# Linear attention on one core: K and V in rows of 8 KB, V loaded straight into its blocks, the first matmul 128 wide

## The chip, the cores and the metric

The kernel runs on one core of a Trainium2 chip. The metric is device time in microseconds (us) of one execution. The engines are TensorE (PE; its weight loads are listed as PEld), VectorE (DVE), ScalarE (ACT), GpSimd (POOL) and SyncE (SP). POOL and SP issue the transfers (DMA).

## What is computed

```python
# Q, K, V: (8, 12, 512, 64) float32
Q_feat = np.maximum(0, Q) + 1
K_feat = np.maximum(0, K) + 1
KV = np.einsum('bhkd,bhkv->bhdv', K_feat, V)
K_sum = np.sum(K_feat, axis=2)
numerator = np.einsum('bhqd,bhdv->bhqv', Q_feat, KV)
denominator = np.einsum('bhqd,bhd->bhq', Q_feat, K_sum)
return numerator / (denominator[:, :, :, None] + 1e-10)
```

There are 96 heads (8 x 12) of 512 rows of 64 numbers. Each of Q, K, V and the output is 12.6 MB. For every head a 64x64 matrix KV and a vector K_sum of 64 are formed, and then each query row is multiplied by them and divided.

## The kernel before

**Tiling.** The inputs are read as a list of rows, and a partition of the on-chip memory gets several successive rows. For K and V a partition gets 16 rows (`C2`, 4 KB in HBM) of each of two or four chunks, for Q 32 rows (`C4`, 8 KB). With 16 rows a partition, 32 partitions hold one head, and a chunk of 128 partitions holds four heads. A *group* g (12 of them, `NG`) is two such chunks, eight heads; a *pair* s is two groups, 16 heads, for which one DMA each loads K, V and Q (1 MB as landed, since the loads turn four-byte numbers into two-byte ones on their way; `load`, line 106, and `load_q`, line 112). The first K goes over SP without conversion (`load_first_k`, line 93).

**First product.** A matmul contracts over the partitions, and 128 partitions hold four heads. To keep the heads apart, V is spread: `v_all` has, for each row, four blocks of 64 columns, of which partition 32b..32b+31 fills only block b and holds zeros in the others, and four columns of ones in the same pattern for K_sum. The zeros are written once (`clear`, lines 240 to 242). `v_blocks` copies each loaded V into its blocks with four copies of 32 partitions, three on DVE (line 155) and one on ACT (line 153). `k_features` forms max(K+1, 1) on DVE (line 137). `keys_values` (line 171) runs, for each of the 16 rows, two matmuls of 64 stationary columns and 260 moving ones: chunk 0 goes to PSUM partitions 0 to 63, chunk 1 to 64 to 127. ACT copies the result out into `kva_all` (lines 181 and 182), in which the two heads that share a column block stand on a diagonal with zeros beside them.

**Queries.** `q_features` (line 137 again, two instructions a group) and `transposes` (line 192: 16 matmuls with an identity a group, in two PSUM tiles, each copied out by ACT at line 195; one of them by DVE near the end).

**Output.** `output(g)` is two halves; in each, 16 matmuls (line 205) write two PSUM tiles of eight, and DVE normalises each tile with a reciprocal (line 222) and a multiplication (line 223) into `o_sb`. Stores of 1 MB (`store`) go over POOL (line 126), the last three over SP (lines 129 and 132).

**Order.** All is written out by hand under `tc.manual_schedule()`: each engine runs its instructions in the order of the program text, and waits for the others by semaphores. In the loop over g, the features and V blocks of group g come before the output of group g-2, then the transposes or Q features, the product of g, and on odd g the loads of the pair after next. Two buffers each for K, V and Q (`IN_BUFS`) set when a load can be issued: the buffer's last reader has to be done. POOL issues its transfers one after the other in that order, and one queue serves them. There are two PSUM tiles each for the product, the output and the transposes, so the third output tile waits until the first has been normalised.

Of the kernel before, what the change touches and what calls it, by code (L numbers as in the profile page):

```python
# [8 lines left out]
FP32 = mybir.dt.float32  # L9
BF16 = mybir.dt.bfloat16  # L10
ALU = mybir.AluOpType

BANK = 512
IN_BUFS = 2
OUT_BUFS = 3
LAG = 3
# [3 lines left out]
def kernel(  # L20
# [10 lines left out]

# [3 lines left out]
    P = 128  # L43
    C = 8
    C2 = 2 * C
    C4 = 4 * C
    R = 4
    NPAIR = B * H * S // (P * C)
    NP = 4
    NG = NPAIR // NP  # L50
    D1 = D + 1
    W = 2 * D1

    def view(t, c):
        return t.flatten_outer_dims().rearrange("(n p c) d -> p n c d", p=P, c=c)

    q_eights = view(Q, C4)
    k_dram = view(K, C2)
    v_dram = view(V, C2)
# [3 lines left out]
    head_pool = ctx.enter_context(tc.tile_pool(name="head_pool", bufs=1))  # L63
    in_pool = ctx.enter_context(tc.tile_pool(name="in_pool", bufs=IN_BUFS))
    kf_pool = ctx.enter_context(tc.tile_pool(name="kf_pool", bufs=2))
    qf_pool = ctx.enter_context(tc.tile_pool(name="qf_pool", bufs=3))
# [8 lines left out]
    NV = 4  # L75
    v_all = const.tile([P, 2, 2, C2, 4 * D1], BF16, name="v_all")
    ones = const.tile([P, 4], BF16, name="ones")
    zero = const.tile([P, 1], FP32, name="zero")
    kva_all = const.tile([P, NV, 4, 2, D1], BF16, name="kva_all")
    kva_diag = [kva_all[:, i] for i in range(NV)]  # L80

    drams = dict(k=k_dram, v=v_dram)
    raw = {}
    bufs = {}
# [4 lines left out]
    cells_of = {}  # L89

    def load_first_k():
        k_raw = head_pool.tile([P, 2, C2, D], FP32, name="k_first")
        nc.sync.dma_start(out=k_raw, in_=k_dram[:, 0:4:2])
        raw["k", 0] = k_raw

    def load(x, groups):
        s = groups[0] // 2
        if groups[0] % 2 == 0 or (x, s) not in bufs:
            bufs[x, s] = in_pool.tile([P, 4, C2, D], BF16, name=f"{x}_raw")
        if len(groups) == 2:  # L100
            ms = slice(0, 4)
            of = slice(4 * s, 4 * s + 4)
        else:
            ms = slice(groups[0] % 2, 4, 2)
            of = slice(4 * s + groups[0] % 2, 4 * s + 4, 2)
        nc.gpsimd.dma_start(out=bufs[x, s][:, ms], in_=drams[x][:, of])  # L106
        for g in groups:
            raw[x, g] = bufs[x, s][:, g % 2 : 4 : 2]

    def load_q(s):  # L110
        t = in_pool.tile([P, 2, C4, D], BF16, name="q_raw")
        nc.gpsimd.dma_start(out=t, in_=q_eights[:, 2 * s : 2 * s + 2])  # L112
        rows = t.rearrange("p n (r c) d -> p n r c d", c=C)
        for e in range(2):
            raw["q", 2 * s + e] = rows[:, :, :, 4 * e : 4 * e + 4]

    def load_pair(s):
        load("k", (2 * s, 2 * s + 1))
        load("v", (2 * s, 2 * s + 1))
        load_q(s)  # L120

    def store(g):
        s = g // 2
        o_to = o_dram[:, 2 * NP * s : 2 * NP * s + 2 * NP]
        if g < NG - 2:
            nc.gpsimd.dma_start(out=o_to[:, g % 2 : 2 * NP : 2], in_=outs[s][:, g % 2 : 2 * NP : 2])  # L126
            return
        if g == NG - 2:
            nc.sync.dma_start(out=o_to[:, 0 : 2 * NP : 2], in_=outs[s][:, 0 : 2 * NP : 2])
            return  # L130
        for h in range(2):
            nc.sync.dma_start(
                out=o_to[:, 2 * h + g % 2 : 2 * NP : NP], in_=outs[s][:, 2 * h + g % 2 : 2 * NP : NP]
            )

    def feature(dst, src):
        nc.vector.tensor_scalar(  # L137
            out=dst, in0=src, scalar1=1.0, scalar2=1.0, op0=ALU.add, op1=ALU.max
        )

    def k_features(g):
        k_raw = raw.pop(("k", g))
        kf = kf_pool.tile([P, C2, 2, D], BF16, name="kf")
        for n in range(2):
            feature(kf[:, :, n], k_raw[:, n])
        kfs[g] = kf

    def v_blocks(g):
        v_raw = raw.pop(("v", g))
        for b in range(4):  # L150
            ps = slice(32 * b, 32 * b + 32)
            if b == 3:
                nc.scalar.copy(out=v_all[ps, g % 2, :, :, b * D : b * D + D], in_=v_raw[ps])  # L153
            else:
                nc.vector.tensor_copy(  # L155
                    out=v_all[ps, g % 2, :, :, b * D : b * D + D], in_=v_raw[ps]
                )

    def q_features(g):
        q_raw = raw.pop(("q", g))  # L160
        qf = qf_pool.tile([P, R, C // 2, 2, D], BF16, name="qf")
        for n in range(2):
            feature(qf[:, :, :, n], q_raw[:, n])
        qfs[g] = qf

    def keys_values(g):
        kf = kfs.pop(g)
        kva_ps = psum_kva.tile([P, 4 * D1], FP32, name="kva_ps")
        for c in range(C2):
            for n in range(2):  # L170
                nc.tensor.matmul(  # L171
                    kva_ps[64 * n : 64 * n + 64],
                    lhsT=kf[:, c, n, :],
                    rhs=v_all[:, g % 2, n, c, :],
                    start=(c == 0),
                    stop=(c == C2 - 1),
                )
        kva = kva_diag[g % NV]
        for n in range(2):
            ps = slice(64 * n, 64 * n + 64)  # L180
            nc.scalar.copy(out=kva[ps, :, n, 0:D], in_=kva_ps[ps, 0 : 4 * D].rearrange("p (b d) -> p b d", b=4))  # L181
            nc.scalar.copy(out=kva[ps, :, n, D], in_=kva_ps[ps, 4 * D : 4 * D1])  # L182

    def transposes(g):
        qf = qfs.pop(g)
        if g % 2 == 0:
            qts[g // 2] = mid_pool.tile([P, C, P, R], BF16, name="qt")
        for half in range(2):
            qt_ps = psum_qt.tile([P, 2, R, P], BF16, name="qt_ps")
            for c in range(2):  # L190
                for r in range(R):
                    nc.tensor.transpose(qt_ps[:, c, r], qf[:, r, 2 * half + c, :, :], identity)  # L192
            copy = nc.vector.tensor_copy if half and g == NG - 2 else nc.scalar.copy
            lo = g % 2 * 4 + 2 * half
            copy(out=qts[g // 2][:, lo : lo + 2], in_=qt_ps.rearrange("p c r q -> p c q r"))  # L195

    def out_matmuls(g, h):
        qt = qts[g // 2]
        kva = kva_diag[(g // 2 * 2 + h) % NV]
        ops = [psum.tile([P, 2, BANK], FP32, tag="ps", name="o_ps") for _ in range(2)]  # L200
        for c in range(C):
            for j in range(2):
                b = 2 * (g % 2) + j
                q = 16 * (4 * h + b)
                nc.tensor.matmul(  # L205
                    ops[c // 4][64 * j : 64 * j + 64, c // 2 % 2, (c % 2) * W : (c % 2) * W + W],
                    lhsT=qt[:, c, q : q + 16, :],
                    rhs=kva[:, b],
                    start=True,
                    stop=True,  # L210
                )
        cells_of[g, h] = ops

    def norms(g, h):
        ops = cells_of.pop((g, h))
        if (g % 2, h) == (0, 0):
            outs[g // 2] = out_pool.tile([P, 2 * NP, C, D], FP32, name="o_sb")
        o_sb = outs[g // 2]
        for i in range(2):
            cells = ops[i][:, :, 0 : 2 * W].rearrange("p b (c n x) -> p b c n x", n=2, x=D1)  # L220
            recip = recip_pool.tile([P, 2, 2, 2, 1], FP32, name="recip")
            nc.vector.reciprocal(out=recip, in_=cells[:, :, :, :, D:D1])  # L222
            nc.vector.tensor_tensor(  # L223
                out=o_sb[:, 2 * h + g % 2 : 2 * NP : NP, 4 * i : 4 * i + 4].rearrange(
                    "p n (b c) d -> p b c n d", b=2
                ),
                in0=cells[:, :, :, :, 0:D],
                in1=recip.to_broadcast([P, 2, 2, 2, D]),
                op=ALU.mult,
            )  # L230

    def output(g):
        for h in range(2):
            out_matmuls(g, h)
            norms(g, h)

    def clear(i):
        t = v_all[:, i].rearrange("p n c x -> p (n c x)").bitcast(FP32)
        w = t.shape[1] * 5 // 8
        nc.vector.memset(t[:, 0:w], 0.0)  # L240
        nc.scalar.copy(out=t[:, w:], in_=zero.to_broadcast([P, t.shape[1] - w]))  # L241
        nc.vector.tensor_copy(
            out=v_all[:, i, :, :, 4 * D : 4 * D1].rearrange("p n c j -> p (n c) j"),
            in_=ones[:, None, :].to_broadcast([P, 2 * C2, 4]),
        )

    with tc.manual_schedule():
        nc.vector.memset(zero, 0.0)
        load_first_k()
        load("v", (0,))  # L250
        load_q(0)
        load("k", (1,))
        load("v", (1,))
# [78 lines left out]
```

## Time and profile before

| What | Value |
|---|---|
| runs (median of 3; lowest to highest) | 126.66 us (126.54 to 127.17) |
| profiled execution, its span | 124.7 us (the page gives the span; the median of the runs lies 1.96 us above it) |
| PE busy | 61.8 us, 960 matmuls |
| DVE busy | 89.3 us |
| ACT busy | 59.6 us |
| POOL busy | 26.1 us |
| bytes over HBM | 37.75 MB read, 12.58 MB written |
| POOL's DMA queue | 10448 packets, 97.4% of 16 DMA engines' span |
| K, V, Q loads, 1 MB landed each | 22.1, 23.0, 26.0 us from issue to landing (median) |
| first K, 1 MB over SP | 4.9 us from issue to landing |

How to read the views used: the page's slices show the span in 40 equal parts, each digit the busy share in tenths (9 is 90% or more); PEclk is the clock that TensorE was granted, in tenths of full speed. The DMA share is that of the 16 DMA engines. A view of stretches gives busy us and the number of instructions for each engine in a stretch of time, then the granted clock, the DMA share and the GB/s as landed. A group line gives source line, engine, operation, output and inputs with their shapes, the count, busy us, mean ns of one, idle time before them and what ended it. In the view in order of time each line begins with the start and the length in us. Matmuls are pipelined, so that the length of one says little: the time in which 32 of them pass says more.

### The profile page before, as it was taken

The page shows a single profiled execution, that of the slowest core. Times are in us where ns is not written, and L with a number is a line of the kernel's source. Part 1 is how long each engine was busy: PE and PEld are TensorE (multiplying, and loading weights), DVE is VectorE, ACT ScalarE, POOL GpSimd, SP SyncE. Part 2 cuts the span into 40 slices and gives each one's busy share as a digit, 9 for nine tenths or more (in the row PEclk, how much of TensorE's full clock was granted, in tenths as well). Part 3 has the DMA queues.
Part 4 walks back from the last instruction along what each step waited for, and adds up shares of the span by engine and source line. Part 5 has one row for each costly group of instructions (what it writes and reads, how often), then busy time and mean ns, then how long its engine had stood idle before and what let it go on. Part 6 is the DMA issues. An engine that isn't in the chain of part 4 may idle for free.

```text
span 124.7 us, 2348 instructions
## 1 busy us (share of the span) xinstructions
PE 61.8 (50%) x960; PEld 50.7 (41%) x960; DVE 89.3 (72%) x191; ACT 59.6 (48%) x86; POOL 26.1 (21%) x51
## 2 busy tenths in 40 slices
PE   0004945200692838539684691069495267775300
PEld 0003735200581827428573490058384155663100
DVE  4895444206999899997999930699959699969700
ACT  7532289306039781956639462601993295450000
POOL 6991023100011630233302420302020200020000
PEclk9999999955589999995999689756999958997555
DMA  3999999999999999999999999999999999999993
GB/s 95 330 214 214 209 198 210 210 214 213 208 213 213 216 214 208 212 213 217 230 405 327 210 212 214 215 338 403 227 212 215 218 255 415 420 413 416 406 409 126
DMA packets 11803, 32.13 MB, mean 258 GB/s; under 512 B 528, under 2 KB 528, under 8 KB 11792
## 3 DMA queue, kind: packets, MB, share of 16 engines
q0 software_dynamic: 10448, 28.84, 97.4%
q1 hardware_dynamic: 1344, 3.15, 6.7%
q8 instruction: 7, 0.11, 0.3%
q14 instruction: 4, 0.03, 0.1%
HBM read 37.75 MB, written 12.58 MB: 404 GB/s over the span
## 4 chain that ended last, share of the span: by engine, by line
DMA 56%; DVE 19%; PE 8%; ACT 6%; issue 3%; POOL 2%; POOLq 0%
DMA v_raw<-in_V_dram 30%; DMA q_raw<-in_Q_dram 26%; DVE o_sb L223 8%; PE kva_ps L171 5%; DVE v_all L155 5%; ACT v_all L153 3%; DVE qf L137 2%; PE qt_ps L192 2%; DVE recip L222 2%; ACT qt L195 2%; POOL v_raw L106 1%; DVE qt L195 1%; ACT kva_all L181 1%; POOL k_raw L106 1%; DVE kf L137 1%
## 5 line engine op out<-in xcount | busy, mean ns | idle before, releaser
L205 PE MATMUL o_ps<-kva_all,qt 128*64 128x130 bf16 x384 | 20.0, 240 | 37.0 <-DVE recip L222 27.0
L171 PE MATMUL kva_ps<-v_all,kf 128*64 128x260 bf16 x384 | 29.8, 320 | 15.8 <-DVE v_all L155 15.6
L155 DVE COPY v_all<-v_raw 32x2048 bf16<-32x2048 bf16 x36 | 25.8, 717 | 13.5 <-DMA v_raw<-in_V_dram 13.1
L223 DVE TENSOR_TENSOR o_sb<-o_ps,recip 128x512 f32<-128x512 f32 x48 | 33.2, 692 | 1.6
L171 PEld LDWEIGHTS <-kf 128*64 128x64 bf16 x384 | 24.6, 130 | 19.0 <-DVE v_all L155 16.0
L205 PEld LDWEIGHTS <-qt 128*64 128x64 bf16 x384 | 14.0, 118 | 42.2 <-issue 26.0
L153 ACT COPY v_all<-v_raw 32x2048 bf16<-32x2048 bf16 x12 | 22.6, 1893 | 16.9 <-DMA v_raw<-in_V_dram 16.7
L195 ACT COPY qt<-qt_ps 128x1024 bf16<-128x1024 bf16 x23 | 22.2, 1015 | 6.8 <-PE qt_ps L192 6.5
L181 ACT CAST kva_all<-kva_ps 64x256 bf16<-64x256 f32 x24 | 8.9, 371 | 27.5 <-PE kva_ps L171 27.3
L126 POOL DMA_DIRECT2D out_dram<-o_sb x10 | 8.6, 864 | 35.9 <-DVE o_sb L223 27.2
L192 PE MATMUL qt_ps<-identity,qf 128*128 128x128 bf16 x192 | 14.8, 235 | 2.0 <-ACT qt L195 1.3
L192 PEld LDWEIGHTS <-qf 128*128 128x128 bf16 x192 | 12.4, 106 | 4.5 <-issue 2.5
L137 DVE TENSOR_SCALAR kf<-k_raw 128x1024 bf16<-128x1024 bf16 x22 | 8.5, 426 | 7.6 <-DMA k_raw<-in_K_dram 7.6
L106 POOL DMA_DIRECT2D k_raw<-in_K_dram x6 | 4.9, 822 | 35.0 <-DVE kf L137 35.0
L222 DVE RECIPROCAL recip<-o_ps 128x8 f32<-128x8 f32 x48 | 9.6, 200 | 1.4 <-PE o_ps L205 1.2
L137 DVE TENSOR_SCALAR qf<-q_raw 128x1024 bf16<-128x1024 bf16 x24 | 8.8, 431 | 2.1 <-DMA q_raw<-in_Q_dram 2.0
L106 POOL DMA_DIRECT2D v_raw<-in_V_dram x7 | 5.4, 766 | 13.4 <-ACT v_all L153 9.3
L240 DVE MEMSET v_all<- 128x2600 f32 x2 | 4.5, 2225 | 0.9 <-issue 0.9
L112 POOL DMA_DIRECT2D q_raw<-in_Q_dram x6 | 4.3, 716 | 0.0
L182 ACT CAST kva_all<-kva_ps 64x4 bf16<-64x4 f32 x24 | 4.1, 170 | 0.0
L241 ACT COPY v_all<-zero 128x1560 f32<-128x1560 f32 x2 | 2.9, 1487 | 0.0
L261 POOL MEMSET kva_all<- 128x130 bf16 x16 | 2.4, 201 | 0.0
(13 smaller groups left out, 5.8 us busy)
## 6 DMA issues: line engine op xcount, KB each, us to landing
out_dram<-o_sb POOLq DMA_DIRECT2D x10, 1024.0 KB, 25.7
q_raw<-in_Q_dram POOLq DMA_DIRECT2D x6, 1024.0 KB, 26.0
k_raw<-in_K_dram POOLq DMA_DIRECT2D x5, 1024.0 KB, 22.1
v_raw<-in_V_dram POOLq DMA_DIRECT2D x5, 1024.0 KB, 23.0
k_first<-in_K_dram SPq DMA_DIRECT2D x1, 1024.0 KB, 4.9
v_raw<-in_V_dram POOLq DMA_DIRECT2D x2, 512.0 KB, 10.7
out_dram<-o_sb SPq DMA_DIRECT2D x1, 1024.0 KB, 7.0
out_dram<-o_sb SPq DMA_DIRECT2D x2, 512.0 KB, 6.4
```

What stands on the lines that cost most here:

```text
L106: nc.gpsimd.dma_start(out=bufs[x, s][:, ms], in_=drams[x][:, of])
L126: nc.gpsimd.dma_start(out=o_to[:, g % 2 : 2 * NP : 2], in_=outs[s][:, g % 2 : 2 * NP : 2])
L137: nc.vector.tensor_scalar(out=dst, in0=src, scalar1=1.0, scalar2=1.0, op0=ALU.add, op1=ALU.max)
L153: nc.scalar.copy(out=v_all[ps, g % 2, :, :, b * D : b * D + D], in_=v_raw[ps])
L155: nc.vector.tensor_copy(out=v_all[ps, g % 2, :, :, b * D : b * D + D], in_=v_raw[ps])
L171: nc.tensor.matmul(kva_ps[64 * n : 64 * n + 64], lhsT=kf[:, c, n, :], rhs=v_all[:, g % 2, n, c, :], start=(c == 0), stop=(c == C2 - 1),)
L181: nc.scalar.copy(out=kva[ps, :, n, 0:D], in_=kva_ps[ps, 0 : 4 * D].rearrange("p (b d) -> p b d", b=4))
L192: nc.tensor.transpose(qt_ps[:, c, r], qf[:, r, 2 * half + c, :, :], identity)
L195: copy(out=qts[g // 2][:, lo : lo + 2], in_=qt_ps.rearrange("p c r q -> p c q r"))
L205: nc.tensor.matmul(ops[c // 4][64 * j : 64 * j + 64, c // 2 % 2, (c % 2) * W : (c % 2) * W + W], lhsT=qt[:, c, q : q + 16, :], rhs=kva[:, ...
L222: nc.vector.reciprocal(out=recip, in_=cells[:, :, :, :, D:D1])
L223: nc.vector.tensor_tensor(out=o_sb[:, 2 * h + g % 2 : 2 * NP : NP, 4 * i : 4 * i + 4].rearrange("p n (b c) d -> p b c n d", b=2), in0=cell ...
```

## The change

- K and V are read with 32 rows a partition (8 KB), as Q is. A head then takes 16 partitions, a chunk eight heads, and a pair two chunks (six pairs; no groups any more).
- V is loaded by four DMAs of 32 partitions each, straight into the blocks of two large buffers (`v_bufs`, nine blocks; chunk 0 uses blocks 0 to 4, chunk 1 blocks 4 to 8). Block 4, shared, holds the four columns of ones. The copies of `v_blocks` go. The zeros are written once: five blocks by DVE, four by ACT, for each buffer.
- A block of 32 partitions now holds two heads. K's features are formed twice, for the even heads with the partitions of the odd ones at zero, and the reverse, by operands that differ per partition (`shift`, `least`, made by `masks`). The two copies are the 128 stationary columns of one matmul; the moving side is five blocks of 64, 320 columns. `keys_values` runs 32 such matmuls for each chunk, and four ACT copies pick the parts.
- The order in the loop becomes, for pair s: features and product of chunk 0, output 0 of pair s-1, features of chunk 1, Q's features, product of chunk 1, output 1 of pair s-1, loads of pair s+2, a store, the transposes of pair s. Output tiles are of 1 MB with six buffers; all stores are 1 MB, two at the end over SP.

```diff
-    q_eights = view(Q, C4)
-    k_dram = view(K, C2)
-    v_dram = view(V, C2)
+    q_dram = view(Q, ROWS)
+    k_dram = view(K, ROWS)
+    v_dram = view(V, ROWS)
...
+    v_bufs = [const.tile([P, 2 * NB - 1, ROWS, D], BF16, name=f"v_buf{i}") for i in range(2)]
+    kvas = [const.tile([P, 8, 2, D1], BF16, name=f"kva{i}") for i in range(2)]
...
+    def load_v(s):
         for b in range(4):
             ps = slice(32 * b, 32 * b + 32)
+            nc.gpsimd.dma_start(
+                out=v_bufs[s % 2][ps, b : b + NB + 1 : NB], in_=v_dram[ps, 2 * s : 2 * s + 2]
+            )
...
+    def k_features(s, n):
+        k_raw = raw.pop(("k", s, n))
+        kf = kf_pool.tile([P, ROWS, 2, D], BF16, name="kf")
+        for a in range(2):
+            nc.vector.tensor_scalar(
+                out=kf[:, :, a],
+                in0=k_raw,
+                scalar1=shift[:, a : a + 1],
+                scalar2=least[:, a : a + 1],
+                op0=ALU.add,
+                op1=ALU.max,
+            )
...
+    def keys_values(s, n):
+        kf = kfs.pop((s, n))
+        v = v_bufs[s % 2][:, n * (NB - 1) : n * (NB - 1) + NB]
+        kva_ps = psum_kva.tile([P, NB, D], FP32, name="kva_ps")
+        for c in range(ROWS):
+            nc.tensor.matmul(
+                kva_ps,
+                lhsT=kf[:, c].rearrange("p a d -> p (a d)"),
+                rhs=v[:, :, c],
...
+        for s in range(NPAIR):
+            k_features(s, 0)
+            keys_values(s, 0)
+            if s:
+                output(s - 1, 0)
+                if s > 1:
+                    store(s - 2, 1, nc.gpsimd)
+            k_features(s, 1)
+            q_features(s)
+            keys_values(s, 1)
+            if s:
+                output(s - 1, 1)
+            if s + 2 < NPAIR:
+                load_k(s + 2)
+                load_q(s + 2)
+                load_v(s + 2)
+            if s:
+                store(s - 1, 0, nc.gpsimd)
+            transposes(s, 0)
+            transposes(s, 1)
+        s = NPAIR - 1
+        store(s - 1, 1, nc.gpsimd)
+        output(s, 0)
+        store(s, 0, nc.sync)
+        output(s, 1)
+        store(s, 1, nc.sync)
```

In the start-up, `load_first_k`, `load_q(0)` and the load of K's second chunk are issued first; `load_v(0)` stands behind the clearing of the first V buffer, `load_k(1)` and `load_q(1)` behind that, and `load_v(1)` behind the clearing of the second.

## The prediction

> **What bounds the kernel now.** I read the page's slices first, then the HBM line, the chain's shares, the stretches of one kind of transfer, and last the groups and the instructions in order of time.
>
> ```profile
> PE 61.8 (50%) x960; PEld 50.7 (41%) x960; DVE 89.3 (72%) x191; ACT 59.6 (48%) x86; POOL 26.1 (21%) x51
> ...
> PEclk9999999955589999995999689756999958997555
> DMA  3999999999999999999999999999999999999993
> ...
> HBM read 37.75 MB, written 12.58 MB: 404 GB/s over the span
> ...
> DMA 56%; DVE 19%; PE 8%; ACT 6%; issue 3%; POOL 2%; POOLq 0%
> ```
>
> The DMA row is full from the second slice to the next to last, and no engine is near full: the transfers are the bound. Three stretches by kind (last column: GB/s as landed; loads land two-byte, so their HBM bytes are double), first Q (8 KB rows), then K and V (4 KB rows), then stores:
>
> ```profile
> 28.80:31.40 2.60, 0.00 (x0) 0.00 (x0) 2.23 (x4) 1.89 (x1) 0.00 (x0) 0.50 1.07 216
> 48.80:51.40 2.60, 2.46 (x48) 2.08 (x46) 2.60 (x8) 1.33 (x5) 0.00 (x0) 1.00 1.13 213
> 104.00:108.00 4.00, 2.67 (x44) 1.91 (x41) 3.93 (x10) 1.98 (x6) 0.00 (x0) 1.00 1.02 417
> ```
>
> That is 432, 426 and 417 GB/s of HBM bytes: 4 KB rows already move within 1.5% of 8 KB rows. At about 420, the 50.33 MB need 119.8 us; with the first data at 2.7 us (an estimate from the first slice) and the last store's completion, 124.7 us is full. A gain is hardly to be had there; the question is whether compute still hides under 20.0 us of DMA per pair (8.39 MB / 0.42; loads alone 15.0, K, Q and V 5.0 each, two stores 5.0).
>
> **The rows for the sum.** Groups of the page (out<-in, count, busy, mean ns), then instructions in order of time (start, us, engine, line):
>
> ```profile
> L171 PE MATMUL kva_ps<-v_all,kf 128*64 128x260 bf16 x384 | 29.8, 320 | 15.8 <-DVE v_all L155 15.6
> L155 DVE COPY v_all<-v_raw 32x2048 bf16<-32x2048 bf16 x36 | 25.8, 717 | 13.5 <-DMA v_raw<-in_V_dram 13.1
> ...
> L137 DVE TENSOR_SCALAR kf<-k_raw 128x1024 bf16<-128x1024 bf16 x22 | 8.5, 426 | 7.6 <-DMA k_raw<-in_K_dram 7.6
> ```
> ```profile
> 86.78 1.07 PE L192 MATMUL qt_ps<-identity,qf 128*128 128x128 bf16 x16
> ...
> 100.97 3.24 PE L171 MATMUL kva_ps<-v_all,kf 128*64 128x260 bf16 x32 [2.69 <-DVE v_all L155]
> ...
> 108.58 1.98 PE L171 MATMUL kva_ps<-v_all,kf 128*64 128x260 bf16 x32
> 110.39 0.62 PE L205 MATMUL o_ps<-kva_all,qt 128*64 128x130 bf16 x16
> ```
>
> What to see: the mean of 320 ns misleads, since 32 matmuls pass in 1.98 us. Two 64-wide ones run side by side, a pair in 124 ns. After an idle 2.69 us the same 32 take 3.24.
>
> **Part 1, first matmul 128 wide.** The count stays 384 (32 per half pair), but each now fills the array by itself and streams 320 columns. Pairs of 260 columns take 124 ns and pairs of 130 columns 78 (0.62 us / 8): 0.354 ns a column more, so 320 columns take 145 ns. By the transposes (1.07 us / 16 = 67 ns for 128 columns with their weight load), scaled, 167. I take 150, nearer to the same instruction: **4.8 us** per 32, bounds 4.65 and 5.35, where 1.98 stood. It can't fall below 1.98: more columns, and no partner beside it. PE's first product grows from 12 x 1.98 = 24 to 58 us.
>
> **Part 2, V into the blocks.** The copies go: 25.8 us of DVE, 12 x 1.89 of ACT. Both lay beside DMA; alone this saves nothing. V costs 24 POOL issues of about 0.7 us, against 7 now; POOL is 21% busy. The first V load now waits for the clears: memset of 5120 elements by the 2600 in 2.23 us, 4.4 us; ACT's 4096 by 1560 in 1.49, about 3.8; done near 6 us. Behind it on POOL stand k1, q1, identity, memsets and v1. The queue then still holds k_first, q0 and half of k0 until about 13 us, which covers it; without cover it would cost 3 us once. V's rate with 32 partitions is not in the trace: nothing lost is one end, half the rate (10 us a pair for V) the other. I take nothing, as the landed 213 GB/s would have to fall below 190 to show at all, other terms being longer.
>
> The Trainium skill, "SBUF — State Buffer", "Door 1: The DMA port swizzle", speaks against this: 32 partitions reach 8 of 16 ports, 189 GB/s measured for 1 MiB against 328. No row here has such a transfer. Counting landed bytes, by its 189 V would take 5.5 us a pair, hidden; counting HBM bytes it is the second rival.
>
> **Part 3, K's features twice.** 24 instructions of 2048 elements replace 24 of 1024. The copies of 2048 elements take 0.69 each: 1.4 us for a half pair, against 0.85 now. A per-partition operand may take the fast rate away; that is a rival. With Q's four (1.43, beside half 1's product) and eight normalisations at 0.84, DVE has 10.9 us a pair, under 20. The five mask instructions and the marks (some 0.06 to 0.3 each) stand on DVE before 11 us, ahead of V0's landing at 18.1, and cost nothing.
>
> **Part 4, the order.** This carries the sum. On PE, pair s runs: product of half 0, output 0 of pair s-1, product of half 1, output 1 of pair s-1, transposes of s. DVE runs output 0's normalisations and only then the features of half 1, for which PE waits. From the rows:
> - product half 0: 4.8;
> - output 0: PE starts at 110.39, the fourth normalisation ends at 114.28 (113.59 + 0.69): 3.9;
> - features of half 1: 1.4;
> - product half 1: 4.8;
> - output 1 on PE: 110.39 to the end of the fourth group at 113.08 is 2.7; its DVE rest and the next half's features (3.9 + 1.4 = 5.3) hide beside the last two terms (6.2);
> - transposes: 16 in 1.07, then ACT's copies hold two more groups of 8 (copies from 87.81, 1.93 for two): 3.5.
>
> Sum **21.1 us a pair**, above DMA's 20.0. The engines are no fuller than now; they take turns.
>
> Now the clock. The window 110.40 to 113.80 holds only spaced output matmuls and the granted clock is 0.5 after it:
>
> ```profile
> 96.00:100.00 4.00, 1.25 (x24) 1.00 1.10 216
> 100.00:104.00 4.00, 3.02 (x32) 0.57 1.03 301
> ```
>
> Here too 1.25 us of PE work in 4 is followed by the low clock, and 32 matmuls at 3.24. In the new order PE has, between the two products, 2.7 us of spaced outputs and 2.6 idle: the same thinness. I add 1.6 us a pair, half of the 3.2 us that the low clock would cover (in the trace it lasts 3.4 us when dense work follows). Bounds: 0, and 3.4 if both halves meet it. **22.7 us a pair.** The Trainium skill, "TensorE: Matmul & The Clock Gate", Part 1, has the clock judged by free-running windows of 3.4 us; the trace agrees (its clock records have low stretches of 3.41, 6.83 and 10.24 us).
>
> Loads stay ahead: V of pair s+2 is issued when half 1 of pair s is done, 15 us in, thus 30 us before use, and needs 20.
>
> **The sum.** V0 lands after the same 6.29 MB as now the second V: 18.1 us. Pair 0 has no outputs: 7.0 (4.8 and 2.2 for the low clock at PE's first work, where now 3.68 stands for 1.98) + 4.8 + 3.5 = 33.4, and V1 lands 15.0 after V0, 33.1. Five pairs: 5 x 22.7 = 113.5, to 146.9. Pair 5's outputs: eight normalisations at 0.84 with 0.8 ahead, 7.5. The last store, 1 MB on SP where two halves stand now, 4.9 (the 1 MB k_first took that from issue to landing; stores behind a backlog take 6.4 to 7.0, and here DMA is idle), 0.6 to the end. Span 159.9. The page has the profiled span, 124.7; the median of the runs, 126.66, lies 1.96 above it, which I add: **162 us**.
>
> **Rivals.**
> - *The chain of turns, forecast* (0.74): pair 20.5 (product 4.5, no low clock) to 24.5: 46.4 + 5P + 2 = 151 to 171.
> - *V at half rate* (0.10): DMA 25 us a pair exceeds 22.7. V0 23, then 20 a pair to V3 83, with stores 25 to V5 133; + 22.7 + 13.0 + 2 = 171. Against: K/V land as fast as Q, nothing suggests a limit on the SBUF side. For: no such shape in the trace.
> - *The features lose their rate* (0.07): by the four-byte row (0.78 for 1024) 3.0 instead of 1.4, pair 25, 173; by a normalisation's 692 ns for 512 elements, 5.5, pair 30, 198. Against: two scalars are already in the instruction; only their kind changes.
> - *DMA stays the bound* (0.06): the wide product costs no more than now, pair 15.5. V5 cannot land before 102.8 (2.7 + 42 MB / 0.42, four stores ahead of it), + 15.5 + 13.0 + 2 = 133; up to 138 at pair 20.
> - *Not slower* (0.03): pair 4's outputs and pair 5's features and transposes run ahead of V5. After V5 stay 4.8 + 4.8 + 7.5 + 5.5 = 22.6; with 1% off the loads 101.8 + 22.6 + 2 = 126.4. It decides only where the outputs stand before the product; in PE's stream they stand behind it.
>
> **Numbers.** Runs of this kernel can tell 0.5% from no change. Faster 0.01, within 0.5% 0.02, slower 0.97. The range 149 to 175 holds the forecast, V at half rate and the first price of the features, and leaves out about 0.12.
>
> **What would show it.** Right: DMA well under 9 tenths in the middle, all loads landed some 20 us before use, PE waiting for DVE's kf once a pair, 32 products in 4.7 to 6.5 us, pairs about 22 us apart. Wrong: a full DMA row to 120 us (DMA still bounds), GB/s near 100 in V's stretches (V's rate), k features over 1 us each (their rate), products under 3 us.

## The result, and the profile after

| | before | after |
|---|---|---|
| runs | 126.62 us median of 4 (126.54 to 127.17) | 159.25 us median of 4 (158.23 to 160.07) |
| ratio after / before | | 1.256, 95% interval 1.2505 to 1.2615: slower |
| profiled execution | 126.66 us, span 124.7 | 158.23 us, span 156.5 (1.73 us lie above the span) |
| POOL's DMA queue, share of 16 engines' span | 97.4% (10448 packets) | 77.2% (7776 packets) |
| 32 matmuls of the first product | 1.98 us at the full clock | 4.35 to 4.51 at the full clock, 6.03 to 7.33 in half 1 |

From the page after: busy times, the rows of clock and DMA over 40 slices of 3.9 us, the bytes, the shares of the chain that ended last, and the two groups that the change made longer: the first product and K's features.

```profile
PE 96.7 (62%) x960; PEld 65.3 (42%) x960; DVE 76.9 (49%) x159; ACT 41.6 (27%) x75; POOL 36.6 (23%) x69
...
PEclk9999999999959999559999699997589998799955
DMA  5999999999999999999999799999910702403376
...
HBM read 37.75 MB, written 12.58 MB: 322 GB/s over the span
...
PE 42%; DVE 30%; DMA 10%; ACT 7%; issue 3%; POOL 3%; ACTq 1%
...
L137 PE MATMUL kva_ps<-v_buf,kf 128*128 128x320 bf16 x384 | 66.4, 342 | 32.1 <-DMA v_buf<-in_V_dram 18.3
...
L109 DVE TENSOR_SCALAR kf<-k_raw,shift,least 128x2048 bf16<-128x2048 bf16 x22 | 17.4, 835 | 6.2 <-PE kva_ps L137 6.2
```

The bytes are those of before. But for the first slice and one of 7 tenths, the DMA row is full for 29 slices, to 113 us, and then it is mostly empty: by then the loads are done, and what is left waits for the engines. In the chain DMA fell from 56% to 10%, PE rose from 8% to 42% and DVE from 19% to 30%. None of the engines is near full, so they wait for one another. How, the chain shows for one pair (start, length, engine, tile, line; the lines left out are the steps between):

```profile
54.67 4.35 PE kva_ps L137 x32
59.02 0.37 PE o_ps L173 x8
...
62.16 0.69 DVE o_sb L183
62.85 1.46 DVE kf L109 x2
...
64.36 7.33 PE kva_ps L137 x32
71.69 0.37 PE o_ps L173 x8
...
74.33 0.57 PE qt_ps L160 x8
...
74.97 1.94 ACT qt L161 x2
...
77.56 4.35 PE kva_ps L137 x32
```

From 54.67 to 77.56 the end is handed on without a gap: product of half 0, output with its normalisations, K's features of half 1 (half n is the pair's chunk n), product of half 1 (7.33 where the one before took 4.35), output, transposes, next product. No DMA stands in it.

The same pair in order of time on PE: the idle time in brackets and what ended it.

```profile
54.51 4.51 PE L137 MATMUL kva_ps<-v_buf,kf 128*128 128x320 bf16 x32
58.95 0.64 PE L173 MATMUL o_ps<-kva,qt 128*64 128x130 bf16 x16
60.48 0.42 PE L173 MATMUL o_ps<-kva,qt 128*64 128x130 bf16 x8 [0.90 <-DVE recip L182]
61.23 0.42 PE L173 MATMUL o_ps<-kva,qt 128*64 128x130 bf16 x8 [0.33 <-DVE o_sb L183]
64.36 7.33 PE L137 MATMUL kva_ps<-v_buf,kf 128*128 128x320 bf16 x32 [2.71 <-DVE kf L109]
```

Between the products PE has 1.48 us of work in 5.3 (0.64 + 0.42 + 0.42), and the clock's records show one low stretch a pair, 3.41 or 6.83 us long, that begins there.

The stretches of one kind of transfer (last columns: granted clock, DMA share, GB/s as landed), first Q or K, then V's four DMAs of 32 partitions; then two of 10 us late in the span:

```profile
18.40:22.60 4.20, 4.20 (x19) 2.40 (x18) 0.10 (x1) 0.00 (x0) 1.63 (x3) 1.00 1.07 215
28.20:32.20 4.00, 2.56 (x35) 2.12 (x34) 0.00 (x0) 3.11 (x7) 2.13 (x4) 1.00 1.06 210
```
```profile
104.00:114.00 10.00, 5.97 (x43) 3.37 (x38) 6.18 (x14) 0.66 (x4) 0.75 (x1) 0.68 0.97 343
114.00:124.00 10.00, 7.76 (x95) 5.66 (x93) 4.85 (x10) 4.64 (x8) 0.75 (x1) 0.98 0.27 102
```

V moves at 210 GB/s landed, 420 of HBM bytes, against 215 and 430 for the other loads. From 114 to 124 us DMA is at a quarter.

### The profile page after: what moved, and what is told of

Same layout as the page of the kernel before. It is cut to its first block, busy times and chain, and to the rows that moved or that the text cites. A ratio compares the mean times of both kernels' runs of the same rounds, so it can differ in the third digit from the quotient of the medians.

```text
span 156.5 us, 2331 instructions
## 1 busy us (share of the span) xinstructions
PE 96.7 (62%) x960; PEld 65.3 (42%) x960; DVE 76.9 (49%) x159; ACT 41.6 (27%) x75; POOL 36.6 (23%) x69
## 3 DMA queue, kind: packets, MB, share of 16 engines
q0 software_dynamic: 7776, 28.84, 77.2%
## 4 chain that ended last, share of the span: by engine, by line
PE 42%; DVE 30%; DMA 10%; ACT 7%; issue 3%; POOL 3%; ACTq 1%
PE kva_ps L137 35%; DVE o_sb L183 16%; DMA v_buf<-in_V_dram 10%; ACT qt L161 7%; DVE v_buf L208 5%; DVE kf L109 5%; PE o_ps L173 4%; DVE recip L182 4%; PE qt_ps L160 3%; POOL v_buf L93 2%; POOL kva L236 1%; ACTq L292 1%; DVE ones L228 0%; DVE v_buf L213 0%; DVE shift L200 0%
## 5 line engine op out<-in xcount | busy, mean ns | idle before, releaser
L137 PE MATMUL kva_ps<-v_buf,kf 128*128 128x320 bf16 x384 | 66.4, 342 | 32.1 <-DMA v_buf<-in_V_dram 18.3
L137 PEld LDWEIGHTS <-kf 128*128 128x128 bf16 x384 | 41.8, 111 | 54.1 <-DVE qf L126 18.0
L148 ACT CAST kva<-kva_ps 64x256 bf16<-64x256 f32 x24 | 8.9, 371 | 91.1 <-PE kva_ps L137 90.8
L173 PE MATMUL o_ps<-kva,qt 128*64 128x130 bf16 x384 | 18.6, 228 | 15.1 <-DVE o_sb L183 10.9
L161 ACT COPY qt<-qt_ps 128x1024 bf16<-128x1024 bf16 x24 | 22.6, 1025 | 11.4 <-PE qt_ps L160 11.4
L93 POOL DMA_DIRECT2D v_buf<-in_V_dram x24 | 15.7, 662 | 27.0 <-PE kva_ps L137 23.0
L173 PEld LDWEIGHTS <-qt 128*64 128x64 bf16 x384 | 12.4, 111 | 22.2 <-DVE o_sb L183 14.4
L109 DVE TENSOR_SCALAR kf<-k_raw,shift,least 128x2048 bf16<-128x2048 bf16 x22 | 17.4, 835 | 6.2 <-PE kva_ps L137 6.2
L208 DVE MEMSET v_buf<- 128x5120 f32 x2 | 8.7, 4325 | 2.1 <-issue 2.1
L210 ACT COPY v_buf<-zero 128x4096 f32<-128x4096 f32 x2 | 7.1, 3601 | 0.0
L149 ACT CAST kva<-kva_ps 64x4 bf16<-64x4 f32 x24 | 4.0, 168 | 0.0
L109 DVE TENSOR_SCALAR kf<-o_sb,shift,least 128x2048 bf16<-128x2048 f32 x2 | 2.6, 1350 | 0.0
## 6 DMA issues: line engine op xcount, KB each, us to landing
k_raw<-in_K_dram POOLq DMA_DIRECT2D x5, 1024.0 KB, 10.7
k_raw<-in_K_dram POOLq DMA_DIRECT2D x1, 512.0 KB, 10.7
```

The source lines that it names most:

```text
L93: nc.gpsimd.dma_start(out=v_bufs[s % 2][ps, b : b + NB + 1 : NB], in_=v_dram[ps, 2 * s : 2 * s + 2])
L109: nc.vector.tensor_scalar(out=kf[:, :, a], in0=k_raw, scalar1=shift[:, a : a + 1], scalar2=least[:, a : a + 1], op0=ALU.add, op1=ALU.max,)
L137: nc.tensor.matmul(kva_ps, lhsT=kf[:, c].rearrange("p a d -> p (a d)"), rhs=v[:, :, c], start=(c == 0), stop=(c == ROWS - 1),)
L148: nc.scalar.copy(out=kva[po, a::2, n, 0:D], in_=kva_ps[pi, n : n + 4])
L161: nc.scalar.copy(out=qts[s][:, lo : lo + 2], in_=qt_ps.rearrange("p c r q -> p c q r"))
L173: nc.tensor.matmul(o_ps[64 * t : 64 * t + 64, c // 2, (c % 2) * W : (c % 2) * W + W], lhsT=qt[:, 4 * i + c, 16 * k : 16 * k + 16], rhs=kva ...
```

## The experiments

The theory is that of the prediction: the engines take turns, and the turn in which PE waits for DVE costs the clock as well. The rivals still open after the profile were that the amount of PE's work by itself makes the time, that the features' operands do, and that V's four DMAs or the wide rows take transfer time that the page doesn't show. Each run stands beside runs of the kernel before on the same chip (medians 126.71, 126.83 and 126.67 us).

### 1. Half 1's features ahead of the output

```diff
             keys_values(s, 0)
+            k_features(s, 1)
+            q_features(s)
             if s:
                 output(s - 1, 0)
                 if s > 1:
                     store(s - 2, 1, nc.gpsimd)
-            k_features(s, 1)
-            q_features(s)
             keys_values(s, 1)
```

> Half 1's K features and Q's features are moved ahead of output 0's normalisations on DVE; nothing else changes. Theory (the engines take turns): PE goes from output 0 straight into half 1's product, so 2.7 us of idle, 1.4 us of features and the low clock's 2 us leave each pair; the pair takes 4.4 + 2.6 + 4.4 + 2.6 + 3.2 = 17.3 us, under the 20.0 of its transfers, and DMA sets the pace again until V5 at about 103 us; then 17.3, perhaps 2 for the low clock after the wait, and 12.8 to the end: span 133 to 135, 135 to 137 us measured. Rival (the amount of work: PE's 58 us of first products are simply too much): order does not matter, 158 us. Rival (V's DMAs or the features are slow): no change, 158 us.

Measured: 137.71 us (135.83 to 138.0), ratio 1.0817 (1.0733 to 1.0902); the median lies just above the 135 to 137 that were expected. The same work, two calls moved ahead of the output, gives back 21.5 of the 32.6 us. From its page, clock and DMA:

```profile
PEclk9999999999999999999999999999999999999855
DMA  4999999999999999999999999999999994808285
```

and from PE in order of time:

```profile
67.83 4.51 PE L137 MATMUL kva_ps<-v_buf,kf 128*128 128x320 bf16 x32
74.91 4.52 PE L137 MATMUL kva_ps<-v_buf,kf 128*128 128x320 bf16 x32
85.13 4.51 PE L137 MATMUL kva_ps<-v_buf,kf 128*128 128x320 bf16 x32
...
103.86 4.51 PE L137 MATMUL kva_ps<-v_buf,kf 128*128 128x320 bf16 x32 [1.27 <-DMA v_buf<-in_V_dram]
```

Both halves now take 4.51 or 4.52, the clock's row has no low slice before the end, no product of these waits for features, a pair takes 17.3 us (67.83 to 85.13), and the last pair waits for its V: DMA sets the pace up to there. What is still lost lies behind V5: 30.1 us from 103.86 to the end of the span at 134.0.

### 2. Outputs and transposes ahead of the products

```diff
             k_features(s, 0)
-            keys_values(s, 0)
+            k_features(s, 1)
             if s:
                 output(s - 1, 0)
...
             q_features(s)
-            keys_values(s, 1)
+            transposes(s, 0)
+            transposes(s, 1)
             if s:
                 output(s - 1, 1)
+            keys_values(s, 0)
+            keys_values(s, 1)
```

> In each pair, both outputs of the pair before and the transposes stand before the first products, which wait for V; the loads stand behind the products and the stores behind the loads, as before. Theory: only 2 x 4.4 (6.4 for the first at the low clock), 7.5 and a store are left behind V5's landing at about 103 us; DMA is full to the end, as in the kernel before: span 124 to 126, 125 to 128 us measured, level with the kernel before within 1%. Rival (amount of PE work): 158 us or little less. Rival (V in 32 partitions slows the transfers once they are the bound): V 5 us a pair longer, about 150 us.

Measured: 154.48 us (153.81 to 155.5), ratio 1.2206 (1.2134 to 1.2277): far off. Its DVE and then its PE in order of time show what the expectation had overlooked:

```profile
69.83 1.54 DVE L109 TENSOR_SCALAR kf<-k_raw,shift,least 128x2048 bf16<-128x2048 bf16 x2 [3.29 <-PE kva_ps L137]
74.18 1.54 DVE L109 TENSOR_SCALAR kf<-k_raw,shift,least 128x2048 bf16<-128x2048 bf16 x2 [2.81 <-PE kva_ps L137]
75.63 0.20 DVE L182 RECIPROCAL recip<-o_ps 128x8 f32<-128x8 f32 x1
```
```profile
65.27 8.87 PE L137 MATMUL kva_ps<-v_buf,kf 128*128 128x320 bf16 x64
...
79.80 1.89 PE L160 MATMUL qt_ps<-identity,qf 128*128 128x128 bf16 x16 [1.93 <-DVE qf L126]
```

The features have two buffers. Those of the next pair wait for the products that read them, DVE stands in that wait with the next normalisations behind it, and PE then waits for normalisations and for Q's features. The pair takes 20.8 to 22.4 us (products at 65.27, 86.10, 107.77, 130.13): the turns are back, only other ones. The run says nothing against the theory, but the order that was meant to show a kernel at the floor did not.

### 3. More work on PE, to hold the clock

```diff
         kva_ps = psum_kva.tile([P, NB, D], FP32, name="kva_ps")
+        for c in range(16 if n and s else 0):
+            nc.tensor.matmul(kva_ps, lhsT=identity, rhs=v[:, :, c], start=True, stop=True)
         for c in range(ROWS):
```

> 16 extra matmuls (identity times a V row, overwritten by the product that follows) stand ahead of half 1's product of pairs 1 to 5, where PE idles 2.7 us for the features. They add 16 x 0.136 = 2.2 us of PE work and take nothing away. Theory: the clock stays at full, half 1's product takes 4.4 to 4.5 us in place of 6.0 to 7.3 (mean 6.6), so 5 x 2.1 = 10.6 us less: about 148 us measured. Rival (the long second products come from something else, such as V's or kf's memory being written beside them): no gain, or up to 5 us more where the extra matmuls end late.

Measured: 148.59 us (147.91 to 149.61), ratio 1.1732 (1.1664 to 1.18). In order of time on PE:

```profile
61.21 0.42 PE L175 MATMUL o_ps<-kva,qt 128*64 128x130 bf16 x8 [0.33 <-DVE o_sb L185]
61.56 2.35 PE L137 MATMUL kva_ps<-v_buf,identity 128*128 128x320 bf16 x16
64.34 4.52 PE L139 MATMUL kva_ps<-v_buf,kf 128*128 128x320 bf16 x32 [0.43 <-DVE kf L109]
```

80 matmuls more, 10.7 us less. The product begins as long after that of half 0 as before (54.48 to 64.34, against 54.51 to 64.36), since DVE's turn is as long, but takes 4.52 instead of 7.33. The mean granted clock rises from 0.899 to 0.974. Over the five pairs the half 1 products go from 32.9 to 22.6 us, which is 10.3. The low clock's price is thus shown by itself, and so is its cause: PE's thin stretch ahead of the product.

### 4. The features with constants

Both copies are formed alike, max(K+1, 1): the zeros for the other head are left out.

```diff
-                scalar1=shift[:, a : a + 1],
-                scalar2=least[:, a : a + 1],
+                scalar1=1.0,
+                scalar2=1.0,
```

> K's features take the constants 1.0 and 1.0 in place of the per-partition operands, so that the zeros for the other head are left out of the computation; shapes, layouts and order stay. The features of 2048 elements took 0.81 us in the changed kernel, where the copies of 2048 took 0.68. If the per-partition operands cost the 0.12, each falls to about 0.69 and half 1's features, on the path of five pairs, save 5 x 0.25 = 1.2 us: 158 us. If the cost is the strided write or the read, it stays at 0.81 and 159 us. In no case does it fall by more than 2 us, unless the operands had taken the fast rate away.

Measured: 157.22 us (157.02 to 157.76), ratio 1.24 (1.2346 to 1.2455). The group of its page, where after has 17.4 us and a mean of 835 ns:

```profile
L109 DVE TENSOR_SCALAR kf<-k_raw 128x2048 bf16<-128x2048 bf16 x22 | 14.1, 683 | 6.9 <-PE kva_ps L137 6.9
```

The median of one falls from 0.806 to 0.684 us: per-partition operands cost 0.12 us for 2048 elements, and the fast rate stays. Of that, 0.24 us a pair lie on the path, 1.2 in all. The median gained somewhat more than that (the two ratios differ by 0.016, 2 us, and their intervals nearly touch). Two runs here have the mean granted clock of the profiled run of after, 0.899: they took 157.02 and 157.13 us against its 158.23, 1.1 to 1.2 us less, as the path has it. The other three runs of after had a clock of 0.881 or 0.882, so the rest goes with the clock of those runs; why it was lower there isn't settled. As the cause of 32 us the operands are out.

### 5. Half of the product

Half of the key rows are left out of KV and K_sum; the order stays.

```diff
-        for c in range(ROWS):
+        for c in range(ROWS // 2):
...
-                stop=(c == ROWS - 1),
+                stop=(c == ROWS // 2 - 1),
```

> The first product runs over 16 of the 32 rows; half of the sum over the keys is left out. All else stays, order included. Theory: each product takes 2.2 us (3.3 at the low clock), the pair 2.2 + 3.9 + 1.5 + 3.3 + 2.6 + 3.2 = 16.7, under 20.0: DMA sets the pace to V5 at about 103 us, then 16.7 + 12.8: span 132.5, 134 us measured, far more than the 5 pairs' products alone would show if the transfers did not step in (5 x 5.5 = 27 us less would be 131). Rival (features or V's DMAs): 5 us less or none, 153 to 158 us.

Measured: 137.57 us (136.92 to 137.91), ratio 1.085 (1.0806 to 1.0893). In order of time on PE:

```profile
33.01 4.43 PE L137 MATMUL kva_ps<-v_buf,kf 128*128 128x320 bf16 x16 [3.87 <-DMA v_buf<-in_V_dram]
...
42.92 4.45 PE L137 MATMUL kva_ps<-v_buf,kf 128*128 128x320 bf16 x16 [2.71 <-DVE kf L109]
...
53.24 2.34 PE L137 MATMUL kva_ps<-v_buf,kf 128*128 128x320 bf16 x16
...
60.92 3.85 PE L137 MATMUL kva_ps<-v_buf,kf 128*128 128x320 bf16 x16 [2.71 <-DVE kf L109]
```

The amount matters as the theory has it: 192 matmuls fewer, 21.7 us less. But the wait for DVE stays at 2.71, and half 1 still runs at the low clock, at 3.85 for 16, so that the pair takes 17.4 us (53.24 to 70.60) instead of 16.7. In the first pair with outputs both products ran at the low clock, and it took 20.2 us (33.01 to 53.24). So the chain reached the last pair only at 105.51, some 2.5 us behind V5's landing; that DMA would set the pace there, as the expectation had it, did not come true, and the time is some 3.5 us above the expected 134. By the amount of work alone, 192 matmuls fewer, this run doesn't tell the chain from a sum of PE's work. Experiments 1 and 3 do: in them the same work in another order, and even more work, is faster.

### 6. The outputs between parts of the product

All features of a pair stand first on DVE; the product is cut into four parts of eight matmuls for each half, with one output tile of the pair before behind each part; the last pair's transposes stand ahead of its product.

```diff
             k_features(s, 0)
-            keys_values(s, 0)
...
             k_features(s, 1)
             q_features(s)
-            keys_values(s, 1)
...
+            if last:
+                transposes(s, 0)
+                transposes(s, 1)
+            for n in range(2):
+                for j in range(4):
+                    keys_part(s, n, j, 4)
+                    if s:
+                        output_tile(s - 1, n, j)
```

> All of a pair's features stand first on DVE; on PE each product is cut into four parts of 8 matmuls, and behind each part stands one output tile of the pair before; in the last pair the transposes stand ahead of the products. Same work as the changed kernel. Theory: a pair takes 8.9 + 2.5 + 3.2 = 14.6 to 15 us, under the transfers' 20; after V5's landing at about 103 us are left 11.4 (up to 13 at the low clock), 7.6 of outputs and 5.2: span 127.5 to 129.5, measured 129 to 131.5 us, better than the changed order with features first (137.7), not better than the kernel before. Rival (turns are not all; the features or the copies of ACT hold it): 135 us or more.

Measured: 134.63 us (134.22 to 135.28), ratio 1.0618 (1.0572 to 1.0664), the best of the versions that compute everything. PE in order of time, in the steady part and before the last product:

```profile
33.13 1.25 PE L142 MATMUL kva_ps<-v_buf,kf 128*128 128x320 bf16 x8
34.31 0.42 PE L181 MATMUL o_ps<-kva,qt 128*64 128x130 bf16 x8
...
47.19 0.61 PE L167 MATMUL qt_ps<-identity,qf 128*128 128x128 bf16 x8 [0.68 <-ACT qt L168]
48.10 0.61 PE L167 MATMUL qt_ps<-identity,qf 128*128 128x128 bf16 x8 [0.31 <-ACT qt L168]
48.72 1.25 PE L142 MATMUL kva_ps<-v_buf,kf 128*128 128x320 bf16 x8
```
```profile
83.80 2.29 PE L142 MATMUL kva_ps<-v_buf,kf 128*128 128x320 bf16 x8 [3.98 <-DMA v_buf<-in_V_dram]
...
103.14 1.89 PE L167 MATMUL qt_ps<-identity,qf 128*128 128x128 bf16 x16 [1.43 <-DVE qf L127]
105.33 1.93 PE L167 MATMUL qt_ps<-identity,qf 128*128 128x128 bf16 x16 [0.30 <-ACT qt L168]
107.05 2.29 PE L142 MATMUL kva_ps<-v_buf,kf 128*128 128x320 bf16 x8
```

In the steady part PE waits 1 us a pair, for ACT's copies of the transposes; a pair takes 15.6 us (33.13 to 48.72), below DMA's 20, and pair 4 waits 3.98 us for its V. Most of the 3 to 5 us missed lies at the last pair: its product began at 107.05, behind features and transposes that DVE and PE took up only after pair 3's outputs had ended at 99.4.

### 7. The same with half of the product

As 6, with half of the key rows left out of KV and K_sum.

```diff
-    KROWS = ROWS
+    KROWS = ROWS // 2
```

> The interleaved order with the first product over 16 of 32 rows; half of the sum over the keys is left out. Theory: what the interleaved version has left over the kernel before is the product's length after V5's landing. With 2 x 2.3 us, PE's 7.1 and DVE's eight normalisations leave 7.5 after V5, outputs 7.6: the last normalisation ends near 118.5, before the stores' queue is empty at about 122.8, so DMA is the bound to the end: span 124.5, measured 126 to 127 us, level with the kernel before. Rival (the wide rows or V's four DMAs cost transfer time): it stays above 129 us.

Measured: a median of 128.69 us over ten runs that scatter from 126.69 to 130.53; the ratio of 1.0046 (1.0004 to 1.0088) rests on the five of them below 128.3 us, and by the median of all ten it would be 1.015. Its DMA row, of a run of 127.85 us:

```profile
DMA  3999999999999999999999999999999999997985
```

The row is full to the 36th slice; before, it was full to the 39th. With rows of 8 KB and V's four DMAs the fastest runs (126.69 and 126.88) reach the floor of before (126.83), so neither keeps the kernel from it, and neither gives a gain below it. But the other five runs lie above the 129 us that the expectation left to the rival. What makes them longer is open: their mean granted clocks (0.816 to 0.839) are close to those of the faster ones (0.828 to 0.836).

### 8. The next pair's features formed early

As 6, with the features one pair ahead, to take away the turn that 6 seemed to lose at the end.

```diff
-            k_features(s, 0)
-            k_features(s, 1)
-            q_features(s)
...
             for n in range(2):
                 for j in range(4):
                     keys_part(s, n, j, 4)
                     if s:
                         output_tile(s - 1, n, j)
+                    if n and not j and not last:
+                        q_features(s + 1)
+                if not last:
+                    k_features(s + 1, n)
```

> The interleaved order with one thing moved: the features of the next pair are formed during the pair before (K's behind each half's product, Q's in half 1). Nothing is left out. In the interleaved kernel the last pair's product began at 107.05, behind 2.98 us of K features, 1.42 of Q features and two groups of transposes at the low clock, while the outputs ahead had ended at 99.43 and the last V's transfer had been issued at 83.94, to land near 103. If that turn is what the interleaved kernel lost, the transposes of the last pair follow those of pair 4 at once (from 101.7, 3.4 us at the full clock) and the last product begins near 105 with its first eight matmuls in 1.26 instead of 2.29: span 130.5, median 131.5 to 132 against its 134.63. If the last V is what the last product waits for, the start stays at 107 and the time at 134 to 135. If the features now get between the normalisations and hold up the outputs in every pair, pairs grow beyond 16 us and the time is above 135.

Measured: 136.05 us (135.84 to 136.3), ratio 1.0727 (1.0682 to 1.0773): slower than 6. It is the third case of the expectation, features that hold up the outputs, but only in the last two pairs (20.9 and 23.6 us), and for a reason that the expectation didn't name. DVE, then PE, in order of time:

```profile
94.00 1.77 DVE L110 TENSOR_SCALAR kf<-k_raw,shift,least 128x2048 bf16<-128x2048 bf16 x2 [1.35 <-DMA k_raw<-in_K_dram]
...
98.94 1.43 DVE L127 TENSOR_SCALAR qf<-q_raw 128x1024 bf16<-128x1024 bf16 x4 [2.33 <-DMA q_raw<-in_Q_dram]
100.29 0.20 DVE L190 RECIPROCAL recip<-o_ps 128x8 f32<-128x8 f32 x1
```
```profile
101.27 0.42 PE L181 MATMUL o_ps<-kva,qt 128*64 128x130 bf16 x8 [3.00 <-DVE o_sb L191]
101.61 1.85 PE L167 MATMUL qt_ps<-identity,qf 128*128 128x128 bf16 x16
...
109.08 1.25 PE L142 MATMUL kva_ps<-v_buf,kf 128*128 128x320 bf16 x8
```

K5 landed only near 94 and Q5 near 98.9. Formed early, the features wait on DVE for these loads, the normalisations stand behind them, and PE waits 3.00 us for those. So the reading of 6 was incomplete. By their times from issue to landing, K5, Q5 and V5 were there in 6 at 93.6, 98.6 and 104.0. Q's features began at 102.33 and the product at 107.05, so the turn cost some 3 us, counted from V5. The other 6 us of the span above before (133.5 against 124.7) would then be what has to follow V5 when it arrives at DMA's pace: a product of 64 matmuls with outputs between, eight more outputs, a store. That is an estimate from these times; no run here has an order that saves the 3 us.

## Why the prediction was right

**The bound and its change.** Right: compute turns took the place of DMA, 22.17 us a pair ((143.69 - 32.82) / 5, from the first product of pair 1 to the outputs of pair 5) where 22.7 was predicted. Experiments 1, 3 and 5 each take another part out of the same chain. Experiment 3 gets all of the time that this part had. Experiment 1 gets 21.5 of 24 us (five pairs of 17.3 in place of 22.2), until DMA sets the pace; experiment 5 gets 21.7.

**The terms of the pair** (measured in the trace after; for the product of half 1 the mean of 6.20, 7.33, 6.15, 7.18 and 6.03; the times of the other steps hardly differ from pair to pair):

| Step | predicted | measured |
|---|---|---|
| product half 0 | 4.8 | 4.35 to 4.51 |
| output 0 with normalisations | 3.9 | 3.85 |
| features of half 1 | 1.4 | 1.5 |
| product half 1, with the low clock | 4.8 + 1.6 | 6.58 |
| output 1 on PE | 2.7 | 2.63 |
| transposes | 3.5 | 3.18 |
| sum | 22.7 | 22.2 |

Two terms were mis-sized in opposite directions. "I take 150" ns a matmul was 141 at most (4.51 / 32) and 136 in the chain (4.35 / 32), below even the bound of 145 that came from 0.354 ns a column. That slope was taken from rows of two matmuls side by side; why one that fills the array needs less, no run shows. The low clock cost 2.1 a pair instead of 1.6 (6.58 - 4.5): "half of the 3.2 us" holds where a low stretch ends after 3.41 us, and two of five lasted 6.83. The Trainium skill, "TensorE: Matmul & The Clock Gate", Part 1, has the clock judged by free-running windows of 3.4 us; both lengths agree, one window or two. That 6.4 for the product of half 1 came so near to the measured 6.58 is luck: its two errors partly cancel.

**Features.** 1.4 against 1.5, because of 0.12 us an instruction for the per-partition operands (experiment 4). The rival of lost rates, 3.0 or 5.5 for two, is out.

**V in four DMAs.** "I take nothing" was right: 210 GB/s landed in after, and a full row in experiment 7. The Trainium skill, "SBUF — State Buffer", "Door 1: The DMA port swizzle", gives 189 GB/s for one transfer to 32 partitions; the runs here show 210 by landed bytes, a tenth more, and over twice as much by HBM bytes, so 189 was no limit for these four back to back by either count. What one such transfer alone would do, no run here shows.

**The ends.** V0 landed at 18.07 (18.1 predicted), pair 0 ended at 32.8 (33.4), and from pair 5's outputs to the end it took 12.8 (13.0). The sum of 159.9 for the span is 3.4 too high, of which 2.6 come from the pairs (113.5 against 110.87), 0.6 from pair 0 and 0.2 from the end. The gap above the span was 1.73 instead of 1.96.

**What was to be seen.** Two signs were off. The 32 products were to take 4.7 to 6.5 us; at the full clock they took less (4.35 to 4.51), and two of five at the low clock more (7.18 and 7.33). And the DMA row was not under 9 tenths in the middle. The loads ran ahead of compute and kept it full to 113 us, and the loss stands as a mostly empty queue after that. For the same reason V5, issued at 93.7 with 12.3 us to landing, was there 16 us before its product at 121.92, not some 20.

**The rival on the other side** is partly answered. By it the time is 126.4 where all of the outputs run ahead of V5. In experiment 1 DMA did set the pace to V5, with V5 at 103.86, and the end still took 30.1 us instead of 22.6: pair 4's outputs and pair 5's transposes stood behind it. Experiment 6 shortened that end and stayed 6% above before. Only with half of the product (experiment 7) was the kernel level, and that in half of its runs. Why the product is that long can be counted: before, 16 steps of two matmuls side by side (124 ns a pair) served eight heads; after, 32 steps of one that fills the array (136 ns) serve as many, 2.2 times as long.

## What to carry to other kernels

Where DMA is full and moves 4 KB rows as fast as 8 KB ones (here 426 against 432 GB/s of HBM bytes), wider rows and fewer copies can gain little or nothing, and what they cost on the engines shows as soon as the engines' order becomes a chain. Write that chain down across the engines, one turn after another, and compare it with the bound; a sum of busy times (PE 62%, DVE 49%) hides it, and two calls in another place were worth 21.5 of the 32.6 us lost. But before moving an instruction ahead, ask what it then waits for (a buffer in experiment 2, a load in experiment 8), and who stands behind it on its engine.

## What the runs showed of the hardware that was not expected

- 2.35 us of matmuls without use, in a gap of 2.7 us on PE, shortened the next 32 from 6.58 us (mean) to 4.52: useless work took 10.7 us off the time.
- A tensor-scalar instruction of 2048 two-byte elements takes 0.806 us with two per-partition operands and 0.684 with two constants.
- A matmul of 128x128 by 320 columns takes 136 to 141 ns in a row of 32 at the full clock; at the low clock 8 take 2.29 instead of 1.26.
- Transfers of 256 KB (as landed) to 32 partitions, four back to back on one queue, moved 210 GB/s landed, 2% less than those to 128 partitions (215).
